# A batched matmul with scale and add: the copy and transpose programs of three engines written as loops, at block heads, with other transfer semaphores

## The chip, the cores and the metric

The kernel runs on one core of one Trainium2 chip. The metric is device time in microseconds (us) of one execution. A core has a matrix engine (TensorE, "PE" in the profile, with its weight loads as "PEld"), a vector engine (VectorE, "DVE"), a scalar engine (ScalarE, "ACT"), a general engine (GpSimd, "POOL") and a sync engine (SyncE, "SP"), which here issues every DMA transfer. Each engine runs its own list of instructions; they meet only through semaphores, counters that one engine raises and another waits for.

## The reference

```python
batch, m, k, n = 16, 512, 1024, 768
x          # float32 (16, 512, 1024)
weight     # float32 (1024, 768)
add_value  # float32 (16, 512, 768)
out = (scale * np.matmul(x, weight) + add_value).astype(np.float32)   # scale = 0.1
```

Taken flat, x has 8192 rows. In MB (10^6 bytes) x is 33.55, weight 3.15, add_value 25.17 and out 25.17, which makes 87.03 MB to move.

## The kernel before

**Tiles and rings.** The 8192 rows are 64 tiles of 128 rows. A **move** is four tiles of x (16 moves), a **pair** two tiles (32 pairs). x lands in `xs`, a ring of 16 tiles; add_value lands in `ao`, a ring of 32 tiles, and the result is written over it there and sent out from there. The weight lands once in slots 16 to 23 of `ao` and is cast to bf16.

**The order of transfers** is written out by hand in `STREAM` (line 22): 28 transfers, each a letter (x, w, a for add_value, o for out), the first tile and the count of tiles. `sync_engine` (line 120) issues 27 of them in this order, and line 243 the last one. Since SP issues in order, a transfer whose condition is not met holds all that follow. The conditions are these:

- line 125: the transfer eight places earlier must have landed, because each transfer's semaphore is one of eight `LANES` used in turn;
- lines 126 to 129: an x transfer past tile 15 waits until both copying engines have emptied the slots that it overwrites;
- lines 130 to 135: an add_value transfer waits for the weight casts where it takes their slots, and from tile 32 on for the landing of the output that left from its slots;
- lines 136 and 137: an output waits until its pairs are finished.

**The stages of a tile.** ACT and POOL run `mover` (line 140), each on half of the partitions: for every move they wait for the x transfer and for a free buffer of `va` (two buffers, line 148), then cast fp32 to bf16 in eight copies of four tiles each (line 157). For the moves in `HALVED` (0, 1 and 10) they make sixteen copies of two tiles, so that the first pair is complete earlier. DVE's `turn` (line 169) transposes one pair from `va` to `xt` (line 177); `finish` (line 182) forms scale times product plus add_value for one pair (line 188). The loop of lines 197 to 204 is unrolled: finish a pair, then turn the pair two places on, except that pairs 0 and 24 (`TURN_FIRST`) turn first. PE (line 219) is a loop already: 16 rounds of four tiles, each tile eight weight loads with matmuls of 512 and 256 columns (lines 232 and 207).

In the program before, only PE has a loop in its code; ACT, POOL, DVE and SP have every instruction written out.

## Time and profile before

| what | value |
|---|---|
| time, median of 3 runs | 209.22 us (209.12 to 209.81) |
| time of the profiled execution | 209.87 us |
| its span, first to last instruction | 208.1 us |
| TensorE clock granted, mean | 0.981 |
| busy share of the span: PE, DVE, ACT, POOL | 81%, 59%, 67%, 67% |
| the kernel's DMA queue, share of 16 DMA engines | 97.9% |
| moved | 87.06 MB, mean 418 GB/s |

The profiled execution took 1.77 us more than its span, which is what lies outside the first and the last instruction. It was 0.65 us slower than the median and 0.06 us slower than the slowest of the three runs. A busy share is a mean over the whole span, so the views by time window and the waits say more than this table about what sets the end. A transfer is split over the 16 DMA engines, and "DMA share" is the mean over these 16; a value above 1.00 in a short window comes from placing a packet's bytes and time in windows.

### The profile page before, as it was taken

To read this page: it belongs to the slowest core of one execution; us is meant where nothing else is said; L and a number is where in the kernel's file an instruction comes from. 1 tells how busy PE (TensorE), PEld (TensorE's weight loads), DVE (VectorE), ACT (ScalarE), POOL (GpSimd) and SP (SyncE) were. 2 spreads that over 40 slices of the span, in tenths; PEclk is the share of its full clock that TensorE was granted. 3 is DMA by queue.
4 is the path that set the end of the run, shared out by engine and by line. 5 is a ranking of instruction groups with operands and counts; after the bars stand their busy time and mean duration, and the time that the engine had idled before them with its cause. 6 is when DMAs were issued, how large, how long until landed. Compare 5 with 4: busy or idle time off the path is not lost.

```text
span 208.1 us, 2174 instructions
## 1 busy us (share of the span) xinstructions
PE 167.7 (81%) x1008; PEld 50.4 (24%) x512; DVE 122.9 (59%) x66; ACT 139.3 (67%) x153; POOL 139.9 (67%) x156
## 2 busy tenths in 40 slices
PE   0001994969999999999999999994999999999500
PEld 0000231313333333333333333321333333333100
DVE  0037309646777777777777777738677759776300
ACT  2495199989799896969694069999998969000000
POOL 0399399999799997969694059999999979000000
PEclk9999999999999999999999999999999999999975
DMA  6999999999999999999999999999999999998993
GB/s 249 452 408 447 409 453 444 409 457 403 436 461 409 425 463 416 367 411 439 439 427 438 419 441 450 403 428 447 435 409 432 427 439 449 449 453 364 454 411 161
DMA packets 4035, 87.06 MB, mean 418 GB/s; under 512 B 448, under 2 KB 448, under 8 KB 448
## 3 DMA queue, kind: packets, MB, share of 16 engines
q1 hardware_dynamic: 4032, 87.03, 97.9%
q14 instruction: 3, 0.02, 0.0%
HBM read 61.87 MB, written 25.17 MB: 418 GB/s over the span
## 4 chain that ended last, share of the span: by engine, by line
DMA 43%; PE 25%; POOL 21%; issue 3%; DVE 2%; SPq 1%; POOLq 0%; DVEq 0%
DMA xs<-in_x_dram 31%; POOL va L157 21%; PE mm L232 16%; DMA out_dram<-ao 12%; PE mm L207 9%; DVE xt L177 1%; DVE ao L188 1%; SPq L115 0%; SPq L113 0%; SPq L117 0%; POOLq L150 0%; SPq L106 0%; DVEq L106 0%; SPq L274 0%; SPq L237 0%
## 5 line engine op out<-in xcount | busy, mean ns | idle before, releaser
L232 PE MATMUL mm<-w_bf,xt 128*128 128x512 bf16 x496 | 163.8, 382 | 26.9 <-DVE w_bf L167 19.8
L157 POOL CAST va<-xs 32x1024 bf16<-32x1024 f32 (+1 forms) x152 | 139.7, 919 | 36.8 <-DMA xs<-in_x_dram 22.4
L157 ACT CAST va<-xs 32x1024 bf16<-32x1024 f32 (+1 forms) x152 | 138.0, 908 | 36.6 <-DMA xs<-in_x_dram 23.4
L207 PE MATMUL mm<-w_bf,xt 128*128 128x256 bf16 x512 | 140.2, 274 | 0.8
L232 PEld LDWEIGHTS mm<-w_bf,xt 128*128 128x128 bf16 x512 | 50.4, 98 | 144.6 <-issue 138.7
L177 DVE STREAM_TRANSPOSE xt<-va 128x1024 f32<-128x1024 f32 x32 | 65.2, 2038 | 32.0 <-POOL va L157 30.6
L188 DVE SCALAR_TENSOR_TENSOR ao<-mm,ao 128x1536 f32<-128x1536 f32 x32 | 56.0, 1754 | 42.5 <-PE mm L207 39.4
L167 DVE CAST w_bf<-ao 128x3072 bf16<-128x3072 f32 x2 | 3.8, 1948 | 0.0
L143 ACT ACT_TABLE_LOAD x1 | 1.3, 1283 | 0.9 <-SPq L237 0.9
L260 POOL MEMSET const-float32-0.0<- 128x1 f32 x1 | 0.1, 98 | 0.2 <-issue 0.2
L260 POOL MEMSET const-bfloat16-1.0<- 128x1 bf16 x1 | 0.1, 101 | 0.0
L260 POOL MEMSET const-float32-1.0<- 128x1 f32 x1 | 0.1, 98 | 0.0
L260 POOL MEMSET const-uint8-127<- 128x1 uint8 x1 | 0.1, 98 | 0.0
## 6 DMA issues: line engine op xcount, KB each, us to landing
xs<-in_x_dram SPq DMA_DIRECT2D x6, 4096.0 KB, 20.8
ao<-in_add_value_dram SPq DMA_DIRECT2D x7, 3072.0 KB, 25.2
out_dram<-ao SPq DMA_DIRECT2D x5, 3072.0 KB, 24.8
xs<-in_x_dram SPq DMA_DIRECT2D x4, 2048.0 KB, 13.3
out_dram<-ao SPq DMA_DIRECT2D x1, 6144.0 KB, 33.9
ao<-in_weight_dram SPq DMA_DIRECT2D x1, 3072.0 KB, 14.1
ao<-in_add_value_dram SPq DMA_DIRECT2D x2, 1536.0 KB, 14.6
out_dram<-ao SPq DMA_DIRECT2D x2, 1536.0 KB, 19.8
```

The lines of the kernel that those rows point to most:

```text
L143: eng.preload_act_table(mybir.ActivationFunctionType.Copy)
L157: copy(va[q % VA_BUFS][32 * b:32 * b + 32, t:t + step, a, :], src[32 * a:32 * a + 32, t:t + step, b, :]).then_inc(count, step // 2)
L167: eng.tensor_copy(w_bf[:, h:h + 4, :], ao[:, W_SLOT + h:W_SLOT + h + 4, :]).then_inc(casts, 4)
L177: eng.transpose(xt[:, 2 * half:2 * half + 2, :, :].rearrange("p i c (a m) -> p i c a m", a=4), pairs.rearrange("p i a (k c) -> p i c a k", ...
L188: eng.scalar_tensor_tensor(a, mm[:, q:q + 2, 0:N], float(scale), a, op0=mybir.AluOpType.mult, op1=mybir.AluOpType.add).then_inc(made, 2)
L207: return eng.add_instruction(mybir.InstMatmult(name=nc.get_next_instruction_name(), engine=eng.engine, ins=[eng.lower_ap(weights), eng.low ...
L232: eng.matmul(mm[:, q, 0:CUT], piece, w_bf[:, j, 0:CUT], **flags)
L260: nc = _bacc.Bacc("TRN2", target_bir_lowering=False, num_devices=1)
```

## The change

The program does the same arithmetic on the same tiles with the same `STREAM`. Five things differ.

1. `mover` keeps moves 0 to 3 written out and runs moves 4 to 15 as a loop of three rounds of four moves; the loop's counter is what the waits compare with.
2. `vector_engine` keeps pairs 0 to 7 and 24 to 31 written out and runs pairs 8 to 23 as a loop of four rounds of four pairs. The slot of `ao` in the loop is worked out from the counter.
3. `at_block` asks for the first instruction of ACT's, POOL's and DVE's programs to be at the head of a block of `FETCH` = 128 instructions; the space ahead of it is branched over.
4. The semaphores of transfers: x transfers past tile 15 use four semaphores `x_sem`, by ring slot, and no longer wait for a lane; add_value transfers of tiles 16 to 47 use one semaphore `a_sem`, and each of them after the first waits until the one before it has landed; the other transfers use twelve lanes. DVE raises `a_sem` and `x_sem` at the start to where the loops' waits begin.
5. Move 10 is no longer in `HALVED`. The copying engines count 8 a move in place of 16.

```diff
-LANES = 8
-HALVED = (0, 1, 10)
+LANES = 12
+G = 8
+FETCH = 128
+HALVED = (0, 1)
+LOOPED = (16, 48)
...
+    def landing(t):
+        op, s, n = t
+        if looped(op, s):
+            if op == "x":
+                return x_sem[s % X_SLOTS // MOVE], 16 * (s // X_SLOTS + 1)
+            return a_sem, 16 * (s // G)
+        i = shared.index(t)
+        return lanes[i % LANES], 16 * (i // LANES + 1)
...
-            if mark > 16:
+            if looped(op, s):
+                if op == "x":
+                    moved = 8 * -(-(last - X_SLOTS) // MOVE)
+                    need(by_act, moved)
+                    need(by_pool, moved)
+                else:
+                    assert n == G
+                    if s > LOOPED[0]:
+                        need(sem, mark - 16)
+            elif mark > 16:
                 need(sem, mark - 16)
...
+    def at_block(eng):
+        eng.addr_align(FETCH, offset=0, max_nops=0)
...
+        for q in range(X_SLOTS // MOVE):
+            move(q, MOVE // 2 if q in HALVED else MOVE, carriers("x", MOVE * q, MOVE),
+                 4 + 4 * q if q >= VA_BUFS else None)
+        need = eng.wait_ge
+        with eng.Fori(32, T + 1, X_SLOTS) as i:
+            for q in range(X_SLOTS // MOVE):
+                move(q, MOVE, [(x_sem[q], i)] if x_begun[q] else [], i + (4 * q - 12) if q < 3 else i)
...
+        eng.sem_inc(a_sem, 2 * LOOPED[0] - 16)
+        for sem, n in zip(x_sem, x_begun):
+            if n:
+                eng.sem_inc(sem, 16 * (1 + X_LOOPS - n))
+        turn_known(0)
...
+        turn_known(1)
+        known_pairs(0, LOOPED[0] // 2)
+        with eng.Fori(2 * LOOPED[0], 2 * LOOPED[1], 2 * G) as i:
+            eng.wait_ge(a_sem, i)
+            for r in range(4):
+                eng.wait_ge(done, i + 4 * (r + 1))
+                finish(r, bass.ds((i // (2 * G)) % (A_SLOTS // G), 1))
+                if r % 2 == 0:
+                    eng.wait_ge(by_act, i + 4 * r + 16)
+                    eng.wait_ge(by_pool, i + 4 * r + 16)
+                turn(r + 2)
+        known_pairs(LOOPED[1] // 2, T // 2)
```

More of the change, by code (lines that the diff above doesn't have):

```diff
@@ L83, with looped @@
     lanes = [tc.alloc_semaphore(f"lane{i}") for i in range(LANES)]
-    landed = [(lanes[i % LANES], 16 * (i // LANES + 1)) for i in range(len(stream) - 1)]
+    x_sem = [tc.alloc_semaphore(f"x{i}") for i in range(X_SLOTS // MOVE)]
+    x_begun = [sum(op == "x" and s >= X_SLOTS and s % X_SLOTS == MOVE * k
+                   for op, s, n in stream) for k in range(X_SLOTS // MOVE)]
+    X_LOOPS = T // X_SLOTS - 1
+    a_sem = tc.alloc_semaphore("a")
+    def looped(op, s):
+        return (op == "x" and s >= X_SLOTS) or (op == "a" and LOOPED[0] <= s < LOOPED[1])
+    shared = [t for t in stream[:-1] if not looped(t[0], t[1])]
+    def landing(t):
[6 more added lines that the diff above has]
+        return lanes[i % LANES], 16 * (i // LANES + 1)
+    landed = [landing(t) for t in stream[:-1]]
     by_act, by_pool, pool_go, turned, casts, done, made = (
@@ L123, in sync_engine @@
             last = s + n
-            if mark > 16:
+            if looped(op, s):
[8 more added lines that the diff above has]
+            elif mark > 16:
                 need(sem, mark - 16)
-            if op == "x" and last > X_SLOTS:
-                moved = 16 * -(-(last - X_SLOTS) // MOVE)
-                need(by_act, moved)
-                need(by_pool, moved)
             if op == "a":
@@ L138, in sync_engine, with move @@
             transfer(eng, op, s, n).then_inc(sem, 16)
+    def at_block(eng):
+        eng.addr_align(FETCH, offset=0, max_nops=0)
     def mover(eng, copy, parity, count, go=None):
-        need = engine(eng)
+        at_block(eng)
         if go is None:
             eng.preload_act_table(mybir.ActivationFunctionType.Copy)
-        for q in range(MOVES):
-            for mark in carriers("x", MOVE * q, MOVE):
-                need(*mark)
-            if q >= VA_BUFS:
-                need(turned, TURNED + MOVE * (q - VA_BUFS + 1))
+        need = engine(eng)
+        def move(q, step, marks, freed):
+            for sem, value in marks:
+                need(sem, value)
+            if freed is not None:
+                eng.wait_ge(turned, freed)
             if go is not None:
@@ L152, in mover @@
             src = xs[:, k:k + MOVE, :].rearrange("p i (b k) -> p i b k", b=4)
-            step = MOVE // 2 if q in HALVED else MOVE
             for t in range(0, MOVE, step):
@@ L156, in mover @@
                     for b in range(4):
-                        copy(va[q % VA_BUFS][32 * b:32 * b + 32, t:t + step, a, :],
-                             src[32 * a:32 * a + 32, t:t + step, b, :]).then_inc(count, step // 2)
+                        copied = copy(va[q % VA_BUFS][32 * b:32 * b + 32, t:t + step, a, :],
+                                    src[32 * a:32 * a + 32, t:t + step, b, :])
+                        if step == MOVE or b % 2:
+                            copied.then_inc(count, 1)
+        for q in range(X_SLOTS // MOVE):
[5 more added lines that the diff above has]
+                move(q, MOVE, [(x_sem[q], i)] if x_begun[q] else [], i + (4 * q - 12) if q < 3 else i)
     def vector_engine(eng):
+        at_block(eng)
         need = engine(eng)
+        ao_g = ao.rearrange("p (g t) n -> p g t n", t=G)
         def cast_w(s, n):
@@ L170, in turn @@
             move, half = divmod(pair, 2)
-            moved = 16 * move + (8 * (half + 1) if move in HALVED else 16)
-            need(by_act, moved)
-            need(by_pool, moved)
-            if pair > 1:
-                need(done, 4 * (pair - 1))
             pairs = va[move % VA_BUFS][:, 2 * half:2 * half + 2, :, :].bitcast(fp32)
@@ L180, in turn, with finish @@
             ).then_inc(turned, 2)
-        def finish(pair):
-            for mark in carriers("a", 2 * pair, 2):
-                need(*mark)
-            need(done, 4 * (pair + 1))
-            a = ao[:, slots("a", 2 * pair, 2), :]
+        def finish(pair, at):
             q = 2 * (pair % 2)
+            a = ao_g[:, at, 2 * (pair % 4):2 * (pair % 4) + 2, :]
             eng.scalar_tensor_tensor(
@@ L190, in finish, with turn_known, known_pairs @@
                 op0=mybir.AluOpType.mult, op1=mybir.AluOpType.add).then_inc(made, 2)
-        turn(0)
+        def turn_known(pair):
+            move, half = divmod(pair, 2)
+            moved = 8 * move + (4 * (half + 1) if move in HALVED else 8)
+            need(by_act, moved)
+            need(by_pool, moved)
+            if pair > 1:
+                need(done, 4 * (pair - 1))
+            turn(pair)
+        def known_pairs(first, last):
+            for pair in range(first, last):
+                ahead = pair + 2 < T // 2
+                if ahead and pair in TURN_FIRST:
+                    turn_known(pair + 2)
+                for mark in carriers("a", 2 * pair, 2):
+                    need(*mark)
+                need(done, 4 * (pair + 1))
+                g = pair // 4 % (A_SLOTS // G)
+                finish(pair, slice(g, g + 1))
+                if ahead and pair not in TURN_FIRST:
+                    turn_known(pair + 2)
+        eng.sem_inc(a_sem, 2 * LOOPED[0] - 16)
[3 more added lines that the diff above has]
+        turn_known(0)
         for op, s, n in stream:
@@ L195, in vector_engine @@
                 cast_w(s, n)
-        turn(1)
-        for pair in range(T // 2):
-            ahead = pair + 2 < T // 2
-            if ahead and pair in TURN_FIRST:
-                need(done, 4 * (pair + 1))
-                turn(pair + 2)
-            finish(pair)
-            if ahead and pair not in TURN_FIRST:
-                turn(pair + 2)
+        turn_known(1)
[10 more added lines that the diff above has]
+        known_pairs(LOOPED[1] // 2, T // 2)
     def matmul_again(eng, product, piece, weights, start, stop):
```

## The prediction

> **What bounds the kernel now.** I read the page's busy times and queues first, then the view by time windows at both ends, then the chain of waits, then SP's timeline.

> ```profile
> span 208.1 us, 2174 instructions
> ...
> PE 167.7 (81%) x1008; PEld 50.4 (24%) x512; DVE 122.9 (59%) x66; ACT 139.3 (67%) x153; POOL 139.9 (67%) x156
> ...
> DMA packets 4035, 87.06 MB, mean 418 GB/s; under 512 B 448, under 2 KB 448, under 8 KB 448
> ...
> q1 hardware_dynamic: 4032, 87.03, 97.9%
> q14 instruction: 3, 0.02, 0.0%
> ```

> No computing engine is near the span; the kernel's own queue takes 97.9% of 16 DMA engines' time. It moves 87.03 MB, all that the reference demands, and the change leaves every byte and the order of transfers as they are. The last row is the one that the change can touch: three packets on the instruction queue, 0.02 MB, so 5 to 8 KB each (0.015 to 0.025 MB by three). They share the DMA engines with the data.

> ```profile
> 0.00:1.00 1.00, 0.00 (x0) 0.00 (x0) 0.00 (x0) 0.10 (x1) 0.20 (x4) 1.00 0.00 0
> 1.00:2.00 1.00, 0.00 (x0) 0.00 (x0) 0.00 (x0) 1.00 (x1) 0.00 (x0) 1.00 0.30 66
> ...
> 200.00:204.00 4.00, 0.00 (x0) 0.00 (x0) 0.00 (x0) 0.00 (x0) 0.00 (x0) 0.55 0.96 412
> 204.00:205.00 1.00, 0.00 (x0) 0.00 (x0) 0.00 (x0) 0.00 (x0) 0.00 (x0) 0.50 0.70 295
> 205.00:206.00 1.00, 0.00 (x0) 0.00 (x0) 0.00 (x0) 0.00 (x0) 0.00 (x0) 0.50 0.20 86
> 206.00:207.00 1.00, 0.00 (x0) 0.00 (x0) 0.00 (x0) 0.00 (x0) 0.00 (x0) 0.50 0.03 12
> ```

> The last two columns are the DMA engines' mean share and GB/s. There is no work in the first microsecond and little in the second; then the share stays near 1 to the end. The end is ragged. After 204 us the shares 0.70, 0.20 and 0.03 make 0.93 us for each engine, so 16 engines with equal loads would end at 204.9. But 0.03 x 16 = 0.5 engine-us are worked after 206, so at least one ends no earlier than 206.5, and at most at 207. **Stagger** between the even end and the last engine: 1.6 to 2.1 us, about 1.9. No engine goes idle on the way, so what delays one DMA engine anywhere is never made up: it stands in its end. So the bound is the slowest of 16 DMA engines.

> **Part by part: waits for transfers.** The lanes' waits and the new ones cost only if the DMA engines run dry. The chain gives landings, SP's timeline the issues.

> ```profile
> 36.02 18.36 DMA xs<-in_x_dram
> ...
> 72.52 24.79 DMA out_dram<-ao
> ...
> 97.81 23.76 DMA xs<-in_x_dram
> ```

> ```profile
> 54.00 0.43 SPq L117 DMA_DIRECT2D ao<-in_add_value_dram  x1
> 72.09 0.33 SPq L115 DMA_DIRECT2D xs<-in_x_dram  x1
> 104.65 0.33 SPq L117 DMA_DIRECT2D ao<-in_add_value_dram  x1
> 111.81 0.33 SPq L115 DMA_DIRECT2D xs<-in_x_dram  x1
> ```

> At 418 GB/s a transfer of eight tiles of x (4.19 MB) takes 10.0 us, one of a or o (3.15 MB) 7.5.

> - a24 now waits for a16. x16 landed at 36.02 + 18.36 = 54.4, a16 behind it at about 61.9: a24 leaves then, not at 54.00. What covers it is x24, in the queue until 71.9. Behind a24 on SP stands x32, which leaves at 72.09 in any case. Cost 0; without x24 it would be 7.9.
> - a32 waits for a24, which is in by about 79.4; it leaves after o0 at 72.52 + 24.79 = 97.3 anyway. Cost 0.
> - a40 waits for a32. o8 is in at about 104.8 (97.3 + 7.5), a32 at 112.2, or 111.6 counted back from x40 (97.81 + 23.76 = 121.6, less 10.0). So a40 leaves some 7 us later than 104.65, covered by x40 until 121.6. Behind it stands x48, which would leave at 111.81: at most 0.8 us late (0.4 of wait and a40's own issue), under the same cover. Cost 0.
> - The waits taken away (x on lanes, eight lanes to twelve) release nothing: those issues already wait for copies or landings named above. Gain 0.

> **Move 10 unsplit.** The chain around it, then DVE's timeline:

> ```profile
> 121.75 0.60 POOL va L157
> ...
> 131.76 0.61 POOL va L157
> 132.44 1.03 POOL va L157
> ...
> 140.09 1.05 POOL va L157
> 141.26 2.02 DVE xt L177
> 143.33 0.39 PE mm L232
> ```

> ```profile
> 127.17 2.05 DVE L177 STREAM_TRANSPOSE xt<-va 128x1024 f32<-128x1024 f32 x1 [0.25 <-POOL va L157]
> 130.36 1.76 DVE L188 SCALAR_TENSOR_TENSOR ao<-mm,ao 128x1536 f32<-128x1536 f32 x1 [1.15 <-PE mm L207]
> 132.51 2.07 DVE L177 STREAM_TRANSPOSE xt<-va 128x1024 f32<-128x1024 f32 x1 [0.39 <-POOL va L157]
> ```

> Sixteen short copies take 121.75 to 132.44, 10.7 us; eight long ones 8 x (140.09 - 132.44)/7 = 8.7. So move 10 is complete at 130.5 and move 11 at 139.2, 1.9 earlier. Pair 20 loses its head start: its transpose goes from 127.17 to 130.5, and PE, which finished pair 19 by 130.36, starts it at 132.6, 2.3 us later.

> ```profile
> 151.69 0.27 PE mm L207
> ...
> 162.09 0.27 PE mm L207
> ```

> A round of four tiles is 10.4 us, a pair 5.2. PE then does pairs 20 and 21 until 143.0; DVE finishes pair 20 (137.8 to 139.6) and transposes pair 22 (to 141.6) in time. Pair 22 starts at 143.0, before at 143.33. **Net for PE: 0.3 earlier, for the end 0.** The cover at the end:

> ```profile
> 197.66 0.33 SPq L118 DMA_DIRECT2D out_dram<-ao  x1
> ```

> The last output (1.57 MB, 3.8 us) has to reach the DMA engines by 204.9 - 3.8 = 201.1. At the start data flowed about 1 us after SP began, so it is there at 198.7: 2.4 us of slack. PE would have to be later than that to cost anything.

> **The loops themselves.** ACT's and POOL's code has 48 + 32 copies in place of 152 each, under the block's 128 instructions; ACT and POOL take 2 back edges each, DVE 3. The price of an edge is not in ACT's, POOL's or DVE's rows. The nearest row is PE's, which takes 15:

> ```profile
> L207 PE MATMUL mm<-w_bf,xt 128*128 128x256 bf16 x512 | 140.2, 274 | 0.8
> ...
> L177 DVE STREAM_TRANSPOSE xt<-va 128x1024 f32<-128x1024 f32 x32 | 65.2, 2038 | 32.0 <-POOL va L157 30.6
> L188 DVE SCALAR_TENSOR_TENSOR ao<-mm,ao 128x1536 f32<-128x1536 f32 x32 | 56.0, 1754 | 42.5 <-PE mm L207 39.4
> ```

> All idle time ahead of L207 is 0.8 us, so an edge costs PE at most 0.05. DVE has 5.2 - 2.04 - 1.75 = 1.4 us free in each pair for the slot's arithmetic. The movers' edges delay x transfers, which are issued under covers like those above (x32 leaves at 72.09, with a24 in the queue until 79.4: 7.3 us). Cost 0; with no cover, 7 x 0.05 = 0.35.

> **The block heads** cost a branch and perhaps a wait for code on three engines at about 0.9 us.

> ```profile
> 8.19 1.26 ACT L157 CAST va<-xs 32x512 bf16<-32x512 f32 x2 [6.01 <-DMA xs<-in_x_dram]
> 8.32 1.26 POOL L157 CAST va<-xs 32x512 bf16<-32x512 f32 x2 [7.88 <-DMA xs<-in_x_dram]
> ```

> Neither has work before 8.19 but a table load; cost 0. But code read there passes through DMA engines which start their data between 1 and 2 us; a packet that falls in the second half of that gives one engine its delay anew.

> **Instruction packets** are the one term. The written-out code of ACT, POOL and DVE shrinks to what may fit one block, so I expect the three packets to leave the busy stretch. Their price has no row of its own. From below: 0, if they ride on engines with time to spare. From above: the whole stagger, 1.9. Between: 0.0% of 16 x 208.1 us is under 0.05%, 1.67 us for three, 0.56 each at most; and 8 KB at 418/16 = 26 GB/s are 0.31. I take **one packet on the last engine at 0.56**, as the row nearest to it is the queue's own, and an engine that changes queues loses more than the bare 0.31. [...]

> **Sum**: 209.87 - 0.56 = 209.3 for the profiled execution. That execution lies 0.65 above the median of 209.22, so for the median 208.66, **208.7 us**, -0.27%.

> **Rivals.**

> - *The fetches don't leave, or ride on engines that aren't last.* They move to the start, or the stagger has other causes. 209.2. For: three packets explain at most 1.67 of a stagger of up to 2.1, and only if all ride on one engine. Against: only a delay counts that comes after 2 us.
> - *The whole stagger is theirs.* 209.2 - 1.9 = 207.3. For: nothing else in the page differs between DMA engines that carry equal loads. Against: three packets, 0.56 at most each, need other delays behind them.
> - *Slower: each taken branch reads code anew.* Place: the 7 back edges and 3 block heads, up to 10 reads for 3 now. With the 7 more spread evenly 7 x 0.56/16 = 0.25, all on the last engine 3.9; at half of them there, 2.0: 211.2. It decides from two more on the last engine (1.1 us). For: a packet is delay wherever it rides. Against: PE's 15 edges, with three packets in all. [...]
> - *PE late.* If move 11 isn't early, PE loses its 2.3 us for good and the slack of 2.4 is used up; with 1 us more, 210.2.

> **How the numbers follow.** A difference under 0.3% (0.63 us: faster is under 208.6, slower over 209.8) is about what can't be told from no change here. Forecast 0.48 (0.22 faster, 0.25 same, 0.01 slower, since 208.66 lies beside the bound); no gain 0.22 (0.03, 0.16, 0.03); whole stagger 0.12, all faster; branches 0.14 (0.13 slower, 0.01 same); PE late 0.04 slower. Sums: faster 0.37, same 0.42, slower 0.21. The range goes from the whole stagger, 207.2, to 210.4, into the branches' case; left out are some 0.10 above and 0.04 below. The forecast and the no-gain case alone would give 208.2 to 209.5.

> **What would show it.** Right: no instruction packets in the span, or only at its very start; DMA share after 206 us gone, even end unchanged near 204.9; a24 issued near 62 and a40 near 112 with shares near 1 behind them; pair 20 transposed near 130.5 and PE going on at 143 as before. Wrong: more packets in the q14 row; a share well under 1 in a window after 61 or 112 us; PE's last matmul over 2.4 us later than now; or a ragged end without instruction packets, which would mean that something else staggers the engines.

## The result, and the profile after

The changed kernel takes 209.88 us (median of 22 runs, 209.52 to 210.28), the kernel before in the same runs 209.42 (209.12 to 209.87): a ratio of 1.0021, 95% interval 1.0014 to 1.0028. The change costs about 0.45 us, where the forecast was a gain of 0.56.

The profiled execution of after took 209.89 us, its median; that of before, on which the forecast was built, took 209.87, the slowest of its 22. So the two spans are equal, and a difference of 0.45 us has to be found in where things lie, not in a sum of the page.

The rows of after's page:

```profile
span 208.1 us, 2223 instructions
...
PE 168.7 (81%) x1008; PEld 50.5 (24%) x512; DVE 122.8 (59%) x66; ACT 137.8 (66%) x145; POOL 138.9 (67%) x148
...
DMA packets 4035, 87.06 MB, mean 418 GB/s; under 512 B 448, under 2 KB 448, under 8 KB 448
...
q1 hardware_dynamic: 4032, 87.03, 97.8%
q14 instruction: 3, 0.02, 0.0%
```

There are three instruction packets in the span, as before: they have not left. Both ends by time window:

```profile
0.00:1.00 1.00, 0.00 (x0) 0.00 (x0) 0.00 (x0) 0.00 (x0) 0.20 (x4) 1.00 0.00 0
1.00:2.00 1.00, 0.00 (x0) 0.00 (x0) 0.00 (x0) 0.68 (x1) 0.00 (x0) 1.00 0.39 82
2.00:3.00 1.00, 0.00 (x0) 0.00 (x0) 0.00 (x0) 0.60 (x1) 0.00 (x0) 1.00 0.73 197
3.00:4.00 1.00, 0.00 (x0) 0.00 (x0) 0.00 (x0) 0.00 (x0) 0.00 (x0) 1.00 0.98 410
4.00:5.00 1.00, 0.00 (x0) 0.00 (x0) 0.00 (x0) 0.00 (x0) 0.00 (x0) 1.00 1.02 418
...
204.00:205.00 1.00, 0.00 (x0) 0.00 (x0) 0.00 (x0) 0.00 (x0) 0.00 (x0) 0.50 0.64 270
205.00:206.00 1.00, 0.00 (x0) 0.00 (x0) 0.00 (x0) 0.00 (x0) 0.00 (x0) 0.50 0.12 49
206.00:207.00 1.00, 0.00 (x0) 0.00 (x0) 0.00 (x0) 0.00 (x0) 0.00 (x0) 0.50 0.03 12
```

A window counts the packets that start in it. The DMA engines are not full until about 3 us (share 0.73 between 2 and 3, 0.98 between 3 and 4). The end is as ragged as before: one packet starts after 206 us (0.03 x 16 = 0.5 engine-us, that is, us of one engine), and it ends at 206.74, in the trace of before at 206.89. But fewer are late with it: the packets that start between 205 and 206 take 0.12 x 16 = 1.9 engine-us, against 3.2 before. At the start, the timeline of SP and the copying engines:

```profile
1.85 0.76 SPq L138 DMA_DIRECT2D xs<-in_x_dram  x1
2.66 1.01 SPq L140 DMA_DIRECT2D ao<-in_add_value_dram  x2
...
8.90 7.58 ACT L190 CAST va<-xs 32x512 bf16<-32x512 f32 x12 [6.30 <-DMA xs<-in_x_dram]
9.04 7.22 POOL L190 CAST va<-xs 32x512 bf16<-32x512 f32 x11 [8.60 <-DMA xs<-in_x_dram]
```

The first x transfer, issued at the same 0.94 us, is in 0.7 us later than before (8.90 against 8.19). The last packet of this transfer ends at 8.43 us, 0.76 behind that of the middle one of the 16 DMA engines, before at 7.82, 0.31 behind; the copy starts 0.47 and 0.37 later. So an engine is late from the very first transfer on.

The views have no row for a single packet. The trace holds each with start, time and size, so the following is worked out from it: when the instruction packets ran, all of 8192 bytes, and the data packet that came next on the same engine. In the full stream a packet starts 3 or 4 ns before the end of the one ahead of it on its engine, which tells the engines apart. Times are in us.

```
         starts at   took    next data packet, and what its size usually took
before    58.86 us   0.32    1.33, 0.91
          59.15      0.44    1.28, 0.91
         108.32      0.31    1.45, 0.91
after      1.95      0.39    (first data packet of its engine)
           1.99      0.81    (first data packet of its engine)
           4.52      0.32    1.13, 0.61
```

So in these two traces a packet in the full stream costs its DMA engine 0.73 to 0.85 us: its own 0.31 to 0.44, and 0.37 to 0.54 more for the data packet behind it. The three have moved from 59 and 108 us to the first 5.

### The profile page after: what moved, and what is told of

It reads as the page before. It is cut to its first block, busy times and chain, and to the rows that moved or that the text cites. A ratio compares the mean times of both kernels' runs of the same rounds, so it can differ in the third digit from the quotient of the medians.

```text
span 208.1 us, 2223 instructions
## 1 busy us (share of the span) xinstructions
PE 168.7 (81%) x1008; PEld 50.5 (24%) x512; DVE 122.8 (59%) x66; ACT 137.8 (66%) x145; POOL 138.9 (67%) x148
## 2 busy tenths in 40 slices
DMA packets 4035, 87.06 MB, mean 418 GB/s; under 512 B 448, under 2 KB 448, under 8 KB 448
## 3 DMA queue, kind: packets, MB, share of 16 engines
q1 hardware_dynamic: 4032, 87.03, 97.8%
## 4 chain that ended last, share of the span: by engine, by line
DMA 38%; PE 35%; POOL 13%; DVE 4%; issue 3%; ACT 2%; SPq 1%; DVEq 0%; POOLq 0%
DMA xs<-in_x_dram 23%; PE mm L298 23%; POOL va L190 13%; PE mm L273 12%; DMA out_dram<-ao 10%; DMA ao<-in_add_value_dram 5%; DVE xt L217 2%; DVE ao L225 2%; ACT va L190 2%; SPq L138 0%; SPq L136 0%; DVEq L261 0%; POOLq L184 0%; DVEq L129 0%; DVEq L225 0%
## 5 line engine op out<-in xcount | busy, mean ns | idle before, releaser
L190 ACT CAST va<-xs 32x1024 bf16<-32x1024 f32 (+1 forms) x144 | 136.5, 948 | 37.4 <-DMA xs<-in_x_dram 24.8
L298 PEld LDWEIGHTS mm<-w_bf,xt 128*128 128x128 bf16 x512 | 50.5, 99 | 144.7 <-issue 139.6
L225 DVE SCALAR_TENSOR_TENSOR ao<-mm,ao 128x1536 f32<-128x1536 f32 (+1 forms) x32 | 56.1, 1756 | 43.7 <-PE mm L273 39.3
## 6 DMA issues: line engine op xcount, KB each, us to landing
out_dram<-ao SPq DMA_DIRECT2D x2, 1536.0 KB, 19.8
```

The lines of the kernel that those rows point to most:

```text
L190: copied = copy(va[q % VA_BUFS][32 * b:32 * b + 32, t:t + step, a, :], src[32 * a:32 * a + 32, t:t + step, b, :])
L225: eng.scalar_tensor_tensor(a, mm[:, q:q + 2, 0:N], float(scale), a, op0=mybir.AluOpType.mult, op1=mybir.AluOpType.add).then_inc(made, 2)
L298: eng.matmul(mm[:, q, 0:CUT], piece, w_bf[:, j, 0:CUT], **flags)
```

## The experiments

Theory A was that the block heads cost it, by their early reads; its rivals were that the loops do (B), or the added waits or move 10 (C). Each time is compared with runs of the kernel before on the same chip in the same session.

**Heads taken out: e1_no_heads.**

```diff
-        at_block(eng)    # in mover and in vector_engine
```

> The changed kernel without the three block heads; loops, semaphores, waits and the undivided move 10 stay. Theory A (early reads: the heads bring the three instruction packets to 1.9 to 4.5 us, where they delay the first data): the 0.46 us are gone, 209.4, and the packets lie inside the span later than 10 us, or are gone. Theory B (the loops cost it): no change against the changed kernel, 209.9. Theory C (the added waits or move 10 cost it): 209.9 too.

Measured: 209.47 us, ratio 0.9998 (0.9985 to 1.0011), packets at 58.3, 58.4 and 92.6 us. Loops, waits, semaphores and the undivided move 10 together cost nothing. That speaks for A, and against B and C.

**Heads alone: e2_heads_only.**

```diff
     def mover(eng, copy, parity, count, go=None):
         need = engine(eng)
+        eng.addr_align(128, offset=0, max_nops=0)
...
     def vector_engine(eng):
+        eng.addr_align(128, offset=0, max_nops=0)
```

> The kernel before with the three block heads alone. Theory A: 209.9, with three instruction packets before 5 us; ACT's first copy about 0.7 us later, as in the changed kernel (8.90 against 8.19). More than three packets are possible, since the written-out code of ACT and POOL is longer than one block. Theories B and C: 209.4.

Measured: 209.87, ratio 1.0022 (1.0008 to 1.0036): the whole cost, without a loop in these three programs. Packets at 1.9, 2.5 and 3.7 us, and two more near 132 and 133. That these two come because 152 unlooped copies are more than a block of 128 instructions was the author's expectation; the run shows the packets, not why they come. ACT's first copy is at 8.70.

**Move 10 alone: e3_move10_whole.**

```diff
-HALVED = (0, 1, 10)
+HALVED = (0, 1)
```

> The kernel before with move 10 in eight copies, nothing else. Theories A and B: 209.4, PE going on at about 143.0 with pair 22. Theory C for move 10: 209.6 to 209.9, with a later end of PE.

Measured: 209.55, ratio 0.9998 (0.9984 to 1.0011). It costs nothing.

**The transfers' waits alone: e4_transfer_waits.**

```diff
-LANES = 8
+LANES = 12
...
             if op == "a":
+                if s in (24, 32, 40):
+                    for earlier in carriers("a", s - 8, 8):
+                        need(*earlier)
```

> The kernel before with twelve lanes and with add_value transfers of tiles 24, 32 and 40 waiting for the landing of the one before, nothing else. Theories A and B: 209.4, a24 issued near 62 and a40 near 112. Theory C for the waits: 209.6 to 209.9.

Measured: 209.44, ratio 1.0003 (0.9988 to 1.0017). They cost nothing.

So the heads are the cause. It remains to find what it is about them. They could cost by reading code while the first data arrive (A1), by a packet's delay at any time (A2), or outside the span (A3).

**Heads later: e5_heads_later.**

```diff
         for q in range(X_SLOTS // MOVE):
+            if q == 1:
+                at_block(eng)
...
         turn_known(1)
+        at_block(eng)
         known_pairs(0, LOOPED[0] // 2)
```

> The changed kernel with the heads not at the start of the programs but after move 0 (ACT, POOL) and after the weight casts and pair 1's transpose (DVE). Theory A1 (a head costs because its read meets the first data, before 5 us): 209.4; the three packets lie between about 15 and 30 us. Theory A2 (an instruction packet costs the same wherever it falls): 209.4 or 209.9, with no difference between early and late packets. Theory A3 (the head costs outside the span, by the padding in the program): 209.9 as in the changed kernel.

Measured: 209.80, ratio 1.0017 (1.0007 to 1.0027), packets at 19.6, 19.8 and 26.3 us. The cost stays, so A1 in its plain form falls: it is not the first data alone. ACT's first copy is at 8.28, nearly as early as before (8.19), so the cost doesn't need a late first transfer. A3 isn't needed either: the profiled execution lies 1.75 us above its span (209.85 against 208.1), before 1.77, after 1.79.

**Almost no packets: e6_movers_all_loop.** No heads, and all 16 moves in the loop, none of them in sixteen copies; x0 too lands on one of the `x_sem`. The main lines of the edit are these:

```diff
-HALVED = (0, 1)
+HALVED = ()
...
-        with eng.Fori(32, T + 1, X_SLOTS) as i:
+        first = {q: carriers("x", MOVE * q, MOVE) for q in (1, 3)}
+        with eng.Fori(16, T + 1, X_SLOTS) as i:
             for q in range(X_SLOTS // MOVE):
-                move(q, MOVE, [(x_sem[q], i)] if x_begun[q] else [], i + (4 * q - 12) if q < 3 else i)
+                marks = first.get(q, []) + ([(x_sem[q], i)] if x_begun[q] else [])
+                move(q, MOVE, marks, i + (4 * q - 12) if q < 3 else i)
```

> The changed kernel without heads, and with ACT's and POOL's programs wholly a loop (all 16 moves in four rounds, none in HALVED), so that their code should fit what is loaded before the start. The forecast's term (each packet of ACT or POOL taken out of the busy stretch relieves the last DMA engine by 0.56): 208.9, with DVE's packet alone left. Rival (packets cost nothing that the end shows): 209.4. The first pair is complete later, which the slack of 2.4 us at the end should cover; if not, 210 or more and a later end of PE.

Measured: 209.42 (209.31 to 209.71), ratio 1.0003 (0.9995 to 1.0012). This run decides on the forecast's term. Its page and the last windows:

```profile
q14 instruction: 1, 0.01, 0.0%
```

```profile
204.00:205.00 1.00, 0.00 (x0) 0.00 (x0) 0.00 (x0) 0.00 (x0) 0.00 (x0) 0.50 0.50 209
205.00:206.00 1.00, 0.00 (x0) 0.00 (x0) 0.00 (x0) 0.00 (x0) 0.00 (x0) 0.50 0.06 25
206.00:207.00 1.00, 0.00 (x0) 0.00 (x0) 0.00 (x0) 0.00 (x0) 0.00 (x0) 0.50 0.00 0
```

ACT's and POOL's packets are gone (one is left, VectorE's, at 97 us) and the time doesn't fall. The packets that start after 205 us take 0.06 x 16 = 1 engine-us. They are a single engine's, which works on alone to 206.1 and carries no instruction packet at all.

**Many packets of POOL: e7_pool_six_heads.**

```diff
         for q in range(MOVES):
+            if go is not None and q in (4, 6, 8, 10, 12, 14):
+                eng.addr_align(128, offset=0, max_nops=0)
```

> The kernel before with six block heads in POOL's program alone, ahead of moves 4, 6, 8, 10, 12 and 14, so that POOL reads a block at each. If an instruction packet is a delay of 0.5 to 0.8 us that its DMA engine never makes up, and the packets of one queue ride on one engine: six times that less at most 2 us of stagger, so 211 to 213. If packets spread over engines or cost nothing: 209.4 to 209.9.

Measured: 212.23, ratio 1.0144 (1.0124 to 1.0163), with these rows on the page and at the end:

```profile
q14 instruction: 8, 0.07, 0.1%
```

```profile
204.00:208.00 4.00, 0.00 (x0) 0.00 (x0) 0.00 (x0) 0.00 (x0) 0.00 (x0) 0.50 0.33 138
208.00:209.00 1.00, 0.00 (x0) 0.00 (x0) 0.00 (x0) 0.00 (x0) 0.00 (x0) 0.50 0.06 25
```

Five packets more cost 2.85 us, 0.57 each. At the end one engine works on alone (0.06 x 16 = 1). Followed packet by packet, all six of POOL's ride on this engine, which loses 0.40 to 0.67 with each, and it never makes them up. The bound that the prediction named, the slowest of 16 engines, is shown here.

**VectorE's head alone: e8_head_dve_only.** The changed kernel without `at_block` in `mover`.

> The changed kernel with the head of VectorE's program alone. Theory A1: up to a third of the cost, 209.4 to 209.6, with one packet before 5 us and two near 58. Theory A3: a third, 209.6. If DVE's read were the whole cost: 209.9.

Measured: 209.80, ratio 1.0015 (1.0004 to 1.0025), packets at 4.5, 59.1 and 59.2 us. That is nearly the whole cost, not a third.

**The other two heads: f1_heads_act_pool.** The changed kernel without `at_block` in `vector_engine`.

> The changed kernel with the heads of ACT's and POOL's programs, without that of VectorE's: two packets near 2 us, VectorE's near 95. Theory D (the cost is VectorE's packet coming before 90 us, so that three engines and not two are late when the first outputs begin): 209.4. Theory E (any packet at the start costs): 209.8.

Measured: 209.39, ratio 0.9995 (0.9983 to 1.0008), packets at 1.93, 2.00 and 92.7 us. The other two cost nothing. At 2 us a DMA engine has hardly begun: the share is 0.39 between 1 and 2 us in the windows of after, and 1.02 between 4 and 5.

**One early packet in all: f4_one_early_read.** e6_movers_all_loop with `at_block` at the head of `vector_engine`.

> The kernel with ACT and POOL wholly looped (e6_movers_all_loop), with the head of VectorE's program added: one packet in all, near 4.5 us in place of 97. Theory D, as said for three late engines: 209.4, since only one engine is late. Theory F (a packet is worth more the earlier it comes, since the engine that is last loses again at each change from input to output): 209.6 to 209.8.

Measured: 209.87, ratio 1.0014 (1.0003 to 1.0025), with one read at a block head in the span, at 4.82 us (a second instruction packet on its page has 40 bytes). Its end:

```profile
205.00:206.00 1.00, 0.00 (x0) 0.00 (x0) 0.00 (x0) 0.00 (x0) 0.00 (x0) 0.50 0.12 49
206.00:207.00 1.00, 0.00 (x0) 0.00 (x0) 0.00 (x0) 0.00 (x0) 0.00 (x0) 0.50 0.03 12
```

Where e6 shows 0.00 after 206 us, there is an engine again. One packet, moved from 97 us to 5, costs about 0.3 us over the kernel before, in an interval of 0.1 to 0.5 that takes in the change's 0.45. Theory D, which wanted three late engines, falls.

**Six packets of VectorE, early and late: f2_dve_six_early, f3_dve_six_late.**

```diff
         for pair in range(T // 2):
+            if pair in (2, 3, 4, 5, 6, 7):    # f3: (12, 13, 14, 15, 16, 17)
+                eng.addr_align(128, offset=0, max_nops=0)
```

> The kernel before with six heads in VectorE's program, ahead of pairs 2 to 7 (about 43 to 70 us). By the price of POOL's packets (2.85 us for five more): 212 to 213. Theory F: more than the same six packets between 95 and 122 us, by 0.3 or more.

> The kernel before with six heads in VectorE's program ahead of pairs 12 to 17 (about 95 to 122 us). By the price of POOL's packets: 212 to 213. Theory F: 0.3 or more below the kernel with the six before 70 us; without F, the same within 0.2.

Measured: 215.76 (ratio 1.0304, 1.0280 to 1.0329) with the six between 40 and 71 us, and 215.00 (1.0258, 1.0237 to 1.0279) with the six between 93 and 120. Over the kernel before, which has one and took 209.63 in the runs beside them, that is 6.1 and 5.4 us for five more: 1.2 and 1.1 each, where POOL's cost 0.57. More than half of it is common to all DMA engines: the middle one of the 16 ends at 208.4 and 208.0 us, against 204.9 before. The late landings hold up later transfers: POOL's longest wait for x is 13.8 us in both, against 10.0 before, and the outputs that left at 132.88 us leave at 137.34 and 136.72. The rest is the one engine on which all six ride. With one packet it loses 0.98 to 1.00 us in f2 and 0.67 to 1.00 in f3, so here a packet of VectorE is dearer than one of POOL. The six early ones cost 0.8 more in all than the six late ones, as theory F expected.

**Neither start nor late: g1_one_read_at_65.**

```diff
             for pair in range(first, last):
+                if pair == 6:
+                    at_block(eng)
```

> The kernel with ACT and POOL wholly looped (e6_movers_all_loop, one packet at 97 us: 209.42), with VectorE's head moved ahead of pair 6, so that its one packet comes near 65 us. If every packet of VectorE before the first outputs at 88 us costs (its engine, late already, loses again at the change from input to output): 209.8, as with the packet at 4.8 us (209.87). If only a packet at the start of the stream costs: 209.4.

Measured: 209.90 (209.33 to 210.15), ratio 1.0011 (0.9998 to 1.0023), packet at 63.7 us. The median is that of f4, though the interval just takes in 1; it speaks against the start alone as the cause.

**The same time, POOL's read: g2_pool_read_at_20.** e5_heads_later with POOL's head alone.

> The changed kernel with one head, in POOL's program after move 0: POOL's packet near 20 us, ACT's near 58, VectorE's near 93. If the cost hangs on VectorE's queue alone: 209.4. If any packet costs that comes early in the full stream: 209.8, as with all three heads there (209.80).

Measured: 209.28, ratio 0.9988 (0.9975 to 1.0001), packets at 19.7, 59.1 and 93.4 us. An early packet of POOL costs nothing here: its engine ends 0.50 us behind the middle one, while another, which carries no instruction packet, ends 1.37 behind.

**Read before the data: g3_heads_before_start.**

```diff
+    for eng in (nc.scalar, nc.gpsimd, nc.vector):
+        at_block(eng)
     with tc.tile_critical(no_gpsimd_drain=True):
```

> The changed kernel with its three heads placed just ahead of the part in which the programs begin, so that the engines jump some 0.2 us earlier. If VectorE's read then comes by about 2 us, with the other two, before the DMA engines are full: 209.4 or a little less, with no packet later. If it still comes past 3 us: 209.8.

Measured: 209.44 (209.22 to 209.71), ratio 0.9995 (0.9986 to 1.0004), all three packets between 1.76 and 1.92 us and none after. Its end by windows:

```profile
204.00:205.00 1.00, 0.00 (x0) 0.00 (x0) 0.00 (x0) 0.00 (x0) 0.00 (x0) 0.50 0.55 234
205.00:206.00 1.00, 0.00 (x0) 0.00 (x0) 0.00 (x0) 0.00 (x0) 0.00 (x0) 0.50 0.06 25
206.00:207.00 1.00, 0.00 (x0) 0.00 (x0) 0.00 (x0) 0.00 (x0) 0.00 (x0) 0.50 0.00 0
```

Moving the jumps 0.2 to 0.3 us forward (ACT's from 0.90 to 0.73, VectorE's from 1.06 to 0.76) takes away the change's cost. It gains nothing beyond: the end is that of e6, with the packets of one engine alone after 205.1. No version beat the kernel before clear of its interval.

## Why the prediction was wrong, point by point

To see which engine is last, and since when, this table is worked out from the DMA packets of the traces: how far the last of the 16 engines is behind the middle one when the named transfer ends, in us, one profiled execution each. A column is headed by the transfer (the letter and first tile of `STREAM`) and by about when it ends.

```
                          x4     a24    x32    x56    a56    o60    median time
                         24 us    78     88    142    176    205
before                   0.31   0.87   1.37   1.61   1.99   1.98    209.42 (profiled 209.87)
after                    0.82   0.89   1.35   1.88   1.86   1.87    209.88
f4, one packet at 4.8    1.08   1.16   2.01   2.09   1.95   1.95    209.87
g1, one packet at 64     0.27   1.21   2.00   1.95   1.93   1.93    209.90
e6, one packet at 97     0.23   0.22   0.43   0.61   0.89   1.41    209.42
g3, packets before 2     0.15   0.22   0.31   0.28   0.88   1.36    209.44
f1, two at 2, one at 93  0.36   0.44   0.37   0.56   0.68   1.11    209.39
g2, packets at 20,59,93  0.53   0.55   0.65   0.78   0.88   1.37    209.28
```

Followed engine by engine, these traces show two kinds of late engine. One that carries no instruction packet in the full stream is within 0.4 us of the middle one when x32 ends; it then falls behind until the end, most of it while outputs run, and ends 1.1 to 1.4 behind in all eight, in before and after too (1.32 and 1.35). The other kind carries an instruction packet. It sets the end only where it ends further behind than the first: in before (1.98, the packet at 59.15 us), after, f4 and g1, and not in e6, f1 and g2.

**The bound** (the slowest DMA engine, with no idle time to make up a delay): right, shown by e7: 2.85 us for five packets more, all on the engine that ends alone.

**Waits for transfers, cost 0**: right. The first two rows answer to a24 at 54.00 and x32 at 72.09 before, the other two to a40 at 104.65 and x48 at 111.81:

```profile
62.44 0.33 SPq L140 DMA_DIRECT2D ao<-in_add_value_dram  x1
72.92 0.33 SPq L138 DMA_DIRECT2D xs<-in_x_dram  x1
...
111.83 0.33 SPq L140 DMA_DIRECT2D ao<-in_add_value_dram  x1
112.57 0.33 SPq L138 DMA_DIRECT2D xs<-in_x_dram  x1
```

a24 and a40 leave near 62 and 112 us, as forecast, and e4 shows no cost.

**Move 10, net 0 for the end**: right. DVE's timeline after:

```profile
130.60 2.01 DVE L217 STREAM_TRANSPOSE xt<-va 128x1024 f32<-128x1024 f32 x1 [2.94 <-POOL va L190]
132.54 1.71 DVE L225 SCALAR_TENSOR_TENSOR ao<-mm,ao 128x1536 f32 x1
134.18 2.02 DVE L217 STREAM_TRANSPOSE xt<-va 128x1024 f32<-128x1024 f32 x1
138.31 1.76 DVE L225 SCALAR_TENSOR_TENSOR ao<-mm,ao 128x1536 f32 x1 [2.11 <-PE mm L273]
139.99 2.06 DVE L217 STREAM_TRANSPOSE xt<-va 128x1024 f32<-128x1024 f32 x1
143.39 1.76 DVE L225 SCALAR_TENSOR_TENSOR ao<-mm,ao 128x1536 f32 x1 [1.34 <-PE mm L273]
```

Pair 20 is transposed at 130.6 (forecast 130.5), pair 22 at 140.0 (139.6), and PE is through with pair 21 at 143.4 (143.0). The last output leaves at 197.85, 0.19 later than before, inside the slack of 2.4.

**The loops, cost 0**: right (e1). No back edge read code anew: after has three packets, with 7 edges taken. The slower rival, a read at each taken branch, falls. Each of the three heads is followed by one read of 8192 bytes, at 1.95, 1.99 and 4.52 us; why the back edges make none, no run shows.

**The block heads, cost 0: this is the step that failed, and it set the wrong sign.** It said that a read late in the stretch from 1 to 2 us gives one engine its delay anew; the sum then left that out, and the rival in which the reads move to the start put it at no change, 209.2. What the runs show in its place: the reads of ACT and POOL at 2 us are free (f1), VectorE's comes only at 4.5 us, when the engines are full, and it is the cost: 0.3 us in e8 and in f4, with intervals that take in 0.45. By the table it makes its engine 0.8 to 1.1 late from the first transfers. That engine is still last at 88 us, where the last engine loses another 0.46 to 0.85 in after, f4 and g1, and in all three it stays last to the end. In the trace of before, VectorE's packet came at 108 us, behind that point; its engine ended 1.13 behind, and another was last.

**Instruction packets, -0.56: failed too.** Their price came near (0.57 each for POOL's in e7, against 0.56), but by luck: 0.56 was the bound that a rounded 0.0% left, and followed one by one a packet costs its engine 0.40 to 1.00, more than the bare 0.31 as the prediction held. Their removal gains nothing: g3 and e6, with none or one in the stream, are at 209.4 like the kernel before. Two readings were wrong. First, the stagger of 1.9 us was taken from an execution that proved to be the slowest of 22, and what its end would gain was taken off the median too. The profiled executions of e6 and g3, 209.34 and 209.41, are close to the 209.3 forecast for the profiled one; but the median before was at 209.42 already. Second, all of it was put down to packets that could be removed. The table shows that an engine ends 1.1 to 1.4 behind in e6, g3, f1 and g2 too, where no packet made one so late: in g3, with none in the stream, the last is 0.28 behind at 142 us and 1.36 at the end, after most of the outputs. That is the end that is left when the packets are gone, and the sign that the prediction named for it: a ragged end without instruction packets. A packet costs only what it puts its engine beyond that end.

**What stays open.** Why the last engine loses again at about 88 us is argued, not shown: x32, the last input ahead of the first outputs, ends there, and the DMA engines are slow then, as the two traces' windows show (before first, then after: shares of 0.92 and 1.00, but 319 and 375 GB/s, against 418 over the span). The middle one of the 16 takes 10.42 and 10.21 us for x32, where x24 took it 9.71; the one that is behind takes 10.91 and 10.66.

```profile
84.00:88.00 4.00, 3.95 (x25) 1.17 (x12) 3.27 (x2) 3.90 (x5) 3.76 (x5) 1.00 0.92 319
```

```profile
84.00:88.00 4.00, 3.95 (x26) 1.18 (x12) 3.70 (x2) 3.93 (x4) 3.76 (x5) 1.00 1.00 375
```

Against it stands f2, whose last engine, by then 5.7 us late, lost only 0.2 there. The traces say a little more: an engine that an instruction packet had put 0.70 to 1.21 behind by the end of a24 (eleven in all) lost 0.15 to 0.85 more by the end of x32, and one that was 0.50 to 0.69 behind lost 0.21 at most and mostly caught up. That goes for packets of ACT and POOL too: in e5 an engine with one of theirs, at 19.8 us, ended 1.57 behind. Nor do the runs say why VectorE's packets cost more than POOL's, or why one engine falls behind during the outputs. The table has one execution a kernel, and e2's was the fastest of its 12 (209.21 against a median of 209.87, its last engine 1.3 late at the end); the cause rests on the times above, and the table and the engines followed in it only say how.

## What to carry to other kernels

Here the DMA engines were busy nearly to the end (97.8% of the span), and a read of code in the full stream was a delay of one engine, by 0.73 to 0.85 us in before and after. So where they are that busy, ask when a read comes and on which engine, not only how many there are: one packet moved from 97 to 5 us cost about 0.3 us here, and read at 1.9 us, before the engines were full, it was free. A ragged end in one execution is no sum that can be won back: take the engine that is last out, and look for the next one behind it. And a step for which the text itself names a way to cost something belongs in the sum with that price, or in a rival that ends slower.
